# A prompt's last 16 rows as a masked whole tile of 128, and the products with the samples' states with the state moving, four side by side

## The chip, the cores and the metric

One Trainium2 chip, one of its cores. The metric is the device time of one launch in microseconds (us), the median of several runs. TensorE is called PE in the rows (PEld is its loading of the stationary operand), VectorE DVE, ScalarE ACT, GpSimd POOL, SyncE SP.

## What is computed

One inference step of a two-layer trunk with d_model 1024, for a prompt of 2048 tokens (16 learned meta tokens stand in front of it, so 2064 rows) and for 8 samples of one token each that carry states from earlier. In each layer one input projection feeds three branches, and one output projection with a LayerNorm merges them:

```
u = x @ w_in                                    # 5128 columns
A: y_rg  = RG-LRU(conv(rg_in))       * silu     # a scan over time
B: y_ret = norm(retention(q, k, v))  * silu     # 4 heads of 128
C: y_gdn = norm(gated_delta(q, k, v))* silu     # 4 heads of 128
y = LayerNorm(alpha * x + concat(y_rg, y_ret, y_gdn) @ w_out)

retention, a chunk:   o = ((q k^T) * decay) v + (q * q_dec) S ;  S = s_dec * S + (k * k_dec)^T v
gated delta, a chunk: solve (1 + A) [u, w] = [beta v, beta k e^gc] ; v' = u - w S
                      o = (q e^gc) S + att v' ;  S = S e^g + (k e^(g_last - gc))^T v'
```

A prompt starts with S = 0. A sample has its own S per head (128x128 in float32) in both branches: it needs `S^T q`, and in the delta branch `S^T k` too, and it updates S. Everything is float32; the large projections split each operand into two fp32r parts and add three products.

## The kernel before

The work of a layer is done in two superblocks (`sblock`, from L630): 1024 rows first, then 1040 rows of the prompt and the 8 samples. In each, stages K (the delta branch's keys, four heads), A, B and C run in the order of `STAGES`: a stage projects its slabs of w_in on TensorE in blocks of 512 columns (first superblock) or 384, 384 and 280 columns (second), and the scan, retention or delta work of the stage before is recorded between those matmuls by a pump. Behind both superblocks of a layer comes the output projection, row tile by row tile, and beside it the samples' work (`samples_delta`, `samples_ret`, L1135 to L1220).

Every operation goes through a recorder (`Recorder`, which emits all of them at L273, so that nearly every row of the profile shows that line and is told apart by its tiles). It sets each engine's order once, by a list schedule over estimated costs (`cost`, `order`). The order is fixed when the kernel is built: an engine whose next instruction waits holds up those behind it.

The second superblock has 1040 rows of the prompt: two groups of four tiles of 128 rows, and 16 rows that are left. `tl` (in `sblock`) lists them as `(0, 4, 128), (4, 4, 128), (8, 1, 16)`, the last number being the rows `R` of a tile. All steps of the keys, delta and retention branches slice their operands by `R`, so the products of the 16 rows run with 16 rows or 16 columns of TensorE's array: `pdt` and `pk` (`keys_bg`), `pw`, `pu`, `qk`, `pz`, `pd`, `po`, `pno` (`delta_bg`: `prep`, `chain`, `outs`, `norm`), and `qk`, `po`, `pd`, `pno` (`retention_bg`). A plain product in float32 shows as two MATMUL records (two passes), a transpose or an fp32r product as one.

In the samples' work the state of a head, `sv` (128 x 8 samples x 128), is fetched by one DMA, and for each sample its 128x128 matrix is the stationary operand and one column (retention) or two (delta) are moving: 8 products a head. There are 4 heads, 2 branches and 2 layers, so 16 such groups.

At the start SP's queue fetches the first slab `raw`, the first columns of x (`xraw`), the constants `ct`, then small tensors, and then the next slab and columns. The program gives these transfers eight semaphores in turn, so the ninth can only be issued when the first has landed.

## Time and profile before

| | |
|---|---|
| runs of the kernel before | 3144.42, 3139.70, 3141.41 us; median 3141.41 us |
| the profiled execution's own time | 3134.19 us |
| its span, first to last instruction | 3132.2 us |
| mean granted TensorE clock | 0.996 of full speed |
| busy: TensorE | 3089.2 us, 99% of the span |
| busy: VectorE, ScalarE, GpSimd | 65%, 41%, 22% |
| DMA | 262.96 MB, mean 84 GB/s |

How to read it: a share is busy time over the span. A matmul's duration in a row is its latency, and matmuls overlap; what one costs the engine is the distance from its start to the start of the next. In a timeline row "x9" are nine records in a row, its first number is the start of the first of them, and the second the time until the last one's end. Brackets give idle time before the row and what ended it.

### The profile page before, as it was taken

The page shows a single profiled execution, that of the slowest core. Times are in us where ns is not written, and L with a number is a line of the kernel's source. Part 1 is how long each engine was busy: PE and PEld are TensorE (multiplying, and loading weights), DVE is VectorE, ACT ScalarE, POOL GpSimd, SP SyncE. Part 2 cuts the span into 40 slices and gives each one's busy share as a digit, 9 for nine tenths or more (in the row PEclk, how much of TensorE's full clock was granted, in tenths as well). Part 3 has the DMA queues.
Part 4 walks back from the last instruction along what each step waited for, and adds up shares of the span by engine and source line. Part 5 has one row for each costly group of instructions (what it writes and reads, how often), then busy time and mean ns, then how long its engine had stood idle before and what let it go on. Part 6 is the DMA issues. An engine that isn't in the chain of part 4 may idle for free. (4 is left out here: it accounts for less than half of the span.)

```text
span 3132.2 us, 47396 instructions
## 1 busy us (share of the span) xinstructions
PE 3089.2 (99%) x18876; PEld 2707.9 (86%) x18876; DVE 2038.0 (65%) x3736; ACT 1294.2 (41%) x2732; POOL 678.5 (22%) x651
## 2 busy tenths in 40 slices
PE   8999999999999999999999999999999999999999
PEld 6888888899999999788778888888999999997886
DVE  6976565679756565656469765655897565656564
ACT  4455444543454454311144544444434544543100
POOL 2222132222222231011022222222222222311110
PEclk9999999999999999999999999999999999999999
DMA  4121111321111113555231212112211111136641
GB/s 154 63 70 48 57 50 58 110 82 51 49 54 59 46 57 96 179 175 168 95 115 56 70 48 66 52 57 96 85 50 50 54 59 43 61 92 195 183 145 59
DMA packets 137060, 262.96 MB, mean 84 GB/s; under 512 B 24368, under 2 KB 79600, under 8 KB 136840
## 3 DMA queue, kind: packets, MB, share of 16 engines
q1 hardware_dynamic: 113640, 179.91, 18.5%
q0 software_dynamic: 23200, 80.04, 7.1%
q8 instruction: 148, 2.42, 0.3%
q14 instruction: 72, 0.59, 0.1%
HBM read 195.13 MB, written 65.04 MB: 83 GB/s over the span
## 5 line engine op out<-in xcount | busy, mean ns | idle before, releaser
L273 PE MATMUL pj<-arena 128*128 128x512 f32 (+3 forms) x9760 | 2114.1, 360 | 14.3 <-ACT arena L273 7.6
L273 PEld LDWEIGHTS pj<-arena 128*128 128x128 f32 (+1 forms) x9760 | 1625.5, 187 | 170.6 <-ACT arena L273 8.2
L273 POOL TENSOR_TENSOR arena<-raw,arena 128x1024 fp32r<-128x1024 f32 x159 | 399.5, 2512 | 1077.5 <-ACT arena L273 886.4
L273 ACT CAST arena<-raw 128x1024 fp32r<-128x1024 f32 x180 | 189.0, 1050 | 302.4 <-PE pj L273 163.9
L273 DVE SCALAR_TENSOR_TENSOR stg<-stg,eg,pd 128x128 f32<-128x128 f32 x264 | 90.8, 344 | 117.6 <-PE pd L273 116.4
L273 PE MATMUL pj<-arena,ah 128*128 128x512 f32 x512 | 166.0, 401 | 1.3 <-ACT arena L273 1.3
L273 ACT COPY ur<-pj 128x512 f32<-128x512 f32 (+2 forms) x160 | 80.4, 503 | 146.1 <-PE pj L273 146.0
L273 ACT ACT_TABLE_LOAD x106 | 136.0, 1283 | 4.5 <-DVE vT L273 1.9
L273 ACT COPY sw<-pj 64x512 f32<-64x512 f32 (+2 forms) x160 | 79.9, 500 | 103.2 <-PE pj L273 65.7
L273 PEld LDWEIGHTS pj<-arena,ah 128*128 128x128 f32 x512 | 96.7, 189 | 24.5 <-ACT arena L273 1.8
L273 PE MATMUL pj<-arena,al 128*128 128x512 f32 (+1 forms) x296 | 111.6, 398 | 0.1
L273 ACT ACTIVATE g<-pj 128x512 f32<-128x512 f32 (+2 forms) x120 | 61.8, 515 | 109.9 <-PE pj L273 108.9
L273 PE MATMUL pd<-kv 128*128 128x128 f32 x512 | 99.9, 277 | 3.5 <-DVE kv L273 2.6
L273 PEld LDWEIGHTS pz<-stg,wq 128*128 128x128 f32 x512 | 89.7, 189 | 12.5 <-DVE stg L273 2.7
L273 PE MATMUL pz<-stg,wq 128*128 128x128 f32 x512 | 99.6, 276 | 0.8 <-DVE stg L273 0.4
L273 PEld LDWEIGHTS pd<-kv 128*128 128x128 f32 x512 | 86.8, 190 | 13.7 <-issue 2.8
L273 DVE SCALAR_TENSOR_TENSOR g<-g,pj 128x512 f32<-128x512 f32 (+2 forms) x120 | 69.5, 579 | 39.5 <-ACT g L273 38.5
L273 ACT ACTIVATE wq<-pz,eg 64x128 f32<-64x128 f32 x128 | 44.1, 361 | 122.9 <-DVE kv L273 55.1
L273 PE MATMUL po<-arena,ah 128*128 128x512 f32 x288 | 93.9, 400 | 0.0
L273 ACT CAST bh<-mb 128x512 fp32r<-128x512 f32 x32 | 19.6, 620 | 171.3 <-PE po L273 107.9
L273 DVE SCALAR_TENSOR_TENSOR qT<-ur,gcw,qT 128x1024 f32<-128x1024 f32 (+1 forms) x48 | 75.0, 1562 | 18.4 <-ACT qT L273 18.3
L273 DVE SCALAR_TENSOR_TENSOR kT<-ur,gcw,kT 128x1024 f32<-128x1024 f32 (+1 forms) x48 | 74.0, 1541 | 19.2 <-ACT kT L273 18.7
(388 smaller groups left out, 5057.7 us busy)
## 6 DMA issues: line engine op xcount, KB each, us to landing
raw<-in_win SPq DMA_DIRECT2D x160, 512.0 KB, 3.3
ma<-mix_d SPq DMA_DIRECT2D x31, 512.0 KB, 5.1
mix_d<-g POOLq DMA_DIRECT2D x24, 520.0 KB, 3.3
mix_d<-g POOLq DMA_DIRECT2D x24, 512.0 KB, 3.4
raw<-in_wout SPq DMA_DIRECT2D x24, 512.0 KB, 4.4
xr<-in_x SPq DMA_DIRECT2D x16, 512.0 KB, 5.1
x_d<-yo POOLq DMA_DIRECT2D x16, 512.0 KB, 3.3
sv<-row_d POOLq DMA_DIRECT2D x16, 512.0 KB, 4.7
```

The source lines that it names most:

```text
L273: return lambda *args, **kw: self._r.note(self._n, op, lambda: f(*args, **kw), args, kw)
```

## The change

The 16 rows become a tile of 128 that ends with the prompt, so its first 112 rows repeat rows of the second group and must count for nothing. `tl` now carries a tile's first column (`np_ - 128` for the last). New constants in `cl` do the masking: `tmask` (1 for the last 16 rows) on the gates `gg` and `bt`, `tkdec` and `tdec` for retention's decays, `teps` for its epsilon; they are filled by two memsets on GpSimd and four small DMAs on SP's queue. The delta branch takes the last tile's second half chunk only (`q.cis = (1,)`), whose two products with the state (`wt` and `qT`) become one of 128 columns. Only the last 16 columns of the result are written.

In the samples' work `from_state` makes 32 columns (the needed one or two, and neighbours that are not used) stationary and the state moving, at output partitions 0, 32, 64 and 96 in turn; ScalarE copies the 128x256 result out of PSUM, two transposes bring the columns back, and the rest is as before.

```diff
+    cl = cst.tile([128, 13], F32, name="cl")
+    tmask, tkdec, tdec, teps = cl[:, 0:1], cl[:, 1:5], cl[:, 5:9], cl[:, 9:13]
+
+    def tail_constants():
+        G.memset(cl[:, 0:9], 0.0)
+        G.memset(teps, EPS)
+        a = _C["dret"][0] + 127
+        for dst, src in ((tmask, const[0:16, _C["ones"][0]:_C["ones"][1]]),
+                         (tkdec, const[0:16, _C["kdect"][0]:_C["kdect"][1]]),
+                         (tdec, const[0:16, a:a + 385:128]),
+                         (teps, const[0:16, _C["epsr"][0]:_C["epsr"][1]])):
+            SP.dma_start(dst[112:128], src)
...
-            tl = [(0, 4, 128), (4, 4, 128)] + ([(8, 1, 16)] if samp else [])
+
+
+            tl = [(0, 4, 0), (4, 4, 512)] + ([(8, 1, np_ - 128)] if samp else [])
...
-                    V.tensor_tensor(gg, gg, C("valid").unsqueeze(2).to_broadcast([128, 9, 4]), op=OP.mult)
+                    V.tensor_tensor(gg[:, 8], gg[:, 8], tmask.to_broadcast([128, 4]), op=OP.mult)
...
+                    V.tensor_tensor(bt[:, 8], bt[:, 8], tmask.to_broadcast([128, 4]), op=OP.mult)
...
-                        PE.matmul(pd[:R, :nt, :m], m1r[:R, :R], x[:R, :nt, :m], start=(e == 0), stop=False)
-                    PE.matmul(pd[:R, :nt, :m], identb[:R, :R],
-                              negb[:R, :m].unsqueeze(1).to_broadcast([R, nt, m]), start=False, stop=True)
-                    A.activation(dt[:R, t4:t4 + nt, :m], pd[:R, :nt, :m], AF.Exp)
+                        PE.matmul(pd[:, :nt], m1r, x[:, :nt], start=(e == 0), stop=False)
+                    PE.matmul(pd[:, :nt], identb, negb.unsqueeze(1).to_broadcast([128, nt, 64]), start=False, stop=True)
+                    A.activation(dt[:, t4:t4 + nt], pd[:, :nt], AF.Exp)
...
-                        for o in range(0, R, 64):
-                            c0 = (t4 + i) * 128 + o
-                            PE.matmul(pk[o:o + m, i, :m], kT[:, c0:c0 + m], kT[:, c0:c0 + m],
-                                      start=True, stop=True)
-                    if R == 128:
+                        for o in (0, 64):
+                            cc = slice(c0 + i * 128 + o, c0 + i * 128 + o + 64)
+                            PE.matmul(pk[o:o + 64, i], kT[:, cc], kT[:, cc], start=True, stop=True)
+                    if nt == 4:
                         V.tensor_tensor(ap[:, t4:t4 + 4, h, :], pk, dt[:, t4:t4 + 4], op=OP.mult)
                     else:
-                        V.tensor_tensor(apt[:16, :, h], pk[:16, 0, :16], dt[:16, 8, :16], op=OP.mult)
+                        V.tensor_tensor(apt[:, :, h], pk[96:128, 0, 48:64], dt[96:128, 8, 48:64], op=OP.mult)
...
-                        q.wt, q.at = small("wt", [128, 16]), small("at", [16, 16])
+                        q.wq, q.at, q.cis = gs[0].wq, gs[0].at, (1,)
...
+                        A.copy(ttbd[96:128, 0, 112:128], apt[:, :, h])
+                        G.memset(ttbd[96:128, 0, 96:112], 0.0)
+                        G.tensor_copy(q.wq[:, 0, 2], qT[:, c0 + 64:c0 + 128])
...
-                        PE.matmul(pw[:, i, :R], kk[:R, 0, i], inv_t(i), start=True, stop=True)
-                    if R == 128:
+                        PE.matmul(pw[:, i], kk[:, 0, i], ttbd[:, i], start=True, stop=True)
+                    if nt == 4:
                         A.copy(q.wq[:, :, 0:4:3], pw.rearrange("p t (e c) -> p t e c", e=2))
 
                         G.tensor_copy(kk[64:128, 0], kk[64:128, 1])
                         G.memset(kk[0:64, 0], 0.0)
                         G.memset(kk[64:128, 1], 0.0)
                     else:
-                        A.copy(q.wt, pw[:, 0, :R])
+                        A.copy(q.wq[:, 0, 3], pw[:, 0, 64:128])
...
-                        for ci, (o, n) in enumerate(((0, 64), (64, 64)) if q.R == 128 else ((0, 16),)):
+                        for ci in q.cis:
                             pz = q.pz[i // 2][:, i % 2, ci]
-                            if q.R == 128:
-                                PE.matmul(pz, q.wq[:, i, 2 * ci:2 * ci + 2].rearrange("p e c -> p (e c)"), S,
-                                          start=True, stop=True)
-                            else:
-                                PE.matmul(pz[:16], q.wt, S, start=True, stop=True)
-                                PE.matmul(q.pz[0][:16, 0, 1], qT[:, q.c0:q.c0 + 16], S, start=True, stop=True)
-                            if q.R == 128:
-
-                                V.tensor_tensor(uv[o:, 1, i], uv[o:, 0, i], pz[o:], op=OP.add)
-                            else:
-                                V.tensor_tensor(uv[:n, 1, i], uv[:n, 0, i], pz[:n], op=OP.add)
+                            PE.matmul(pz, q.wq[:, i, 2 * ci:2 * ci + 2].rearrange("p e c -> p (e c)"), S,
+                                      start=True, stop=True)
+
+                            o = 64 * ci if nt == 4 else 0
+                            V.tensor_tensor(uv[o:, 1, i], uv[o:, 0, i], pz[o:], op=OP.add)
                             yield
                             ps = p1("pd")
-                            if q.R == 128:
-                                PE.matmul(ps[:, :128], kk[:, 1 - ci, i], uv[:, 1, i], start=True, stop=True)
-                            else:
-                                PE.matmul(ps[:, :128], kk[:n, 1, i], uv[:n, 1, i], start=True, stop=True)
+                            PE.matmul(ps[:, :128], kk[:, 1 - ci, i], uv[:, 1, i], start=True, stop=True)
...
-                        PE.transpose(pn[:, i, :R], q.o[:R, i], C("swap") if R == 128 else ident[:R, :R])
-                    gv = g[:, c0:c0 + nt * R].rearrange("p (t c) -> p t c", t=nt)
-                    V.scalar_tensor_tensor(out=gv, in0=pn[:, :nt, :R], scalar=VV("nw"), in1=gv,
-                                           op0=OP.mult, op1=OP.mult)
-                    yield
-
-                gs = [alloc(i) for i in range(len(tl))]
+                        PE.transpose(pn[:, i], q.o[:, i], C("swap"))
+                    if nt == 4:
+                        gv = g[:, c0:c0 + 512].rearrange("p (t c) -> p t c", t=4)
+                    else:
+                        pn, gv = pn[:, 0, 112:128], g[:, np_ - 16:np_]
...
+            def from_state(pb, sv, cols, c0, n):
+                pr = pt("psv").rearrange("p (s c) -> p s c", s=4)
+                for b in range(NS):
+                    j = 32 * (b % 4)
+                    PE.matmul(pr[j:j + 32, b // 4], cols[:, c0 + n * b:c0 + n * b + 32], sv[:, 0, b], start=True, stop=True)
+                rw = wk.tile([128, 2, 128], F32, tag="gm", name="rw", bufs=2)
+                A.copy(rw, pr[:, 0:2])
+                for s in range(2):
+                    PE.transpose(pb[:, 128 + 128 * s:256 + 128 * s], rw[:, s], ident)
+                return pb[:, 128:384].rearrange("p (b e) -> p b e", e=32)
...
-                    for b in range(NS):
-                        PE.matmul(pb[:, 16 + 2 * b:18 + 2 * b], sv[:, 0, b], kq[:, h, b], start=True, stop=True)
-                    pv = pb[:, 16:32].rearrange("p (b e) -> p b e", e=2)
+                    pv = from_state(pb, sv, swork, 16 * h, 2)
...
-                    for b in range(NS):
-                        PE.matmul(pb[:, b:b + 1], sv[:, 0, b], qs[:, h, b:b + 1], start=True, stop=True)
-                    V.scalar_tensor_tensor(out=o[:, h], in0=pb[:, 0:8], scalar=GAM[h], in1=o[:, h],
+                    pv = from_state(pb, sv, scol.rearrange("p c e h b -> p (c e h b)"), 128 + 8 * h, 1)
+                    V.scalar_tensor_tensor(out=o[:, h], in0=pv[:, :, 0], scalar=GAM[h], in1=o[:, h],
...
-                        PE.matmul(pa[:R, i, :R], kT[:, cc], qT[:, cc], start=True, stop=True)
-                    V.tensor_tensor(sn[:R, 0, :nt, :R], pa[:R, :nt, :R],
-                                    dret[:R, h, :R].unsqueeze(1).to_broadcast([R, nt, R]), op=OP.mult)
+                        cc = slice(c0 + i * 128, c0 + i * 128 + 128)
+                        PE.matmul(pa[:, i], kT[:, cc], qT[:, cc], start=True, stop=True)
+                    if q.last:
+                        V.scalar_tensor_tensor(out=sn[:, 0, 0], in0=pa[:, 0], scalar=tdec[:, h:h + 1],
+                                               in1=C("minc"), op0=OP.mult, op1=OP.mult)
+                    else:
+                        V.tensor_tensor(sn[:, 0, :nt], pa[:, :nt],
+                                        dret[:, h].unsqueeze(1).to_broadcast([128, nt, 128]), op=OP.mult)
...
-                    kd = C("kdec" if R == 128 else "kdect")[:R, h:h + 1]
-                    A.activation(kv[:R, 0, :nt], pk[:R, :nt], AF.Copy, scale=kd)
+                        PE.transpose(pk[:, i, :], kT[:, c0 + i * 128:c0 + i * 128 + 128], ident)
+                    kd = (tkdec if q.last else C("kdec"))[:, h:h + 1]
...
-                        PE.matmul(po[:R, i], qT[:, cc], S, start=False, stop=True, skip_group_check=True)
+                        cc = slice(c0 + i * 128, c0 + i * 128 + 128)
+                        PE.matmul(po[:, i], qT[:, cc], S, start=False, stop=True, skip_group_check=True)
                         ps = p1("pd")
-                        PE.matmul(ps[:, :128], kv[:R, 0, i], kv[:R, 1, i], start=True, stop=True)
-                        V.scalar_tensor_tensor(out=S, in0=S, scalar=GAM[h] ** R, in1=ps[:, :128],
+                        PE.matmul(ps[:, :128], kv[:, 0, i], kv[:, 1, i], start=True, stop=True)
+                        V.scalar_tensor_tensor(out=S, in0=S, scalar=GAM[h] ** (16 if q.last else 128), in1=ps[:, :128],
                                                op0=OP.mult, op1=OP.add)
...
-                        PE.transpose(pn[:, i, :R], q.sn[:R, 1, i], ident[:R, :R])
-                    nv = q.sn[:, 0, :nt, :R]
-                    A.activation(nv, pn[:, :nt, :R], AF.Identity, scale=VV("gnw")[:, h:h + 1],
-                                 bias=VV("gnb")[:, h:h + 1])
-                    gv = g[:, c0:c0 + nt * R].rearrange("p (t c) -> p t c", t=nt)
+                        PE.transpose(pn[:, i], q.sn[:, 1, i], ident)
+                    nv, pn = q.sn[:, 0, :nt], pn[:, :nt]
+                    gv = g[:, q.c0:q.c0 + nt * 128].rearrange("p (t c) -> p t c", t=nt)
+                    if q.last:
+                        nv, pn, gv = nv[:, 0, 112:128], pn[:, 0, 112:128], g[:, np_ - 16:np_]
```

Two places in TensorE's order and one in SP's. First the delta branch's chain of the 16 rows, first head of layer 0, where `kv`/`attb` rows belong to the second group of tiles, `pj` to the projections, and `tk` holds the 16 rows' keys and values. Before:

```order
L273 MATMUL pd<-kv_1099 128x128
L273 MATMUL po<-kv_1099,attb_102 128x128
L273 MATMUL pj<-arena 128x384 x4
L273 MATMUL pz<-stg_103,wt 16x128
L273 MATMUL pz<-stg_103,qT 16x128
L273 MATMUL pj<-arena 128x280 x5
L273 MATMUL pd<-tk 128x128
L273 MATMUL po<-tk,at 16x128
```

Now:

```order
L273 MATMUL pd<-kv_1099 128x128
L273 MATMUL po<-kv_1099,attb_103 128x128
L273 MATMUL pj<-arena 128x384
L273 MATMUL pj<-arena 128x280 x4
L273 MATMUL pz<-stg_104,wq 128x128
L273 MATMUL pj<-arena 128x280 x6
L273 MATMUL pd<-tk 128x128
L273 MATMUL po<-tk,attb_102 128x128
```

Two `pz` products of 16 columns are one of 128, and the last product gives 128 rows instead of 16; the place in the order is nearly the same.

Second, the first delta group of the samples in layer 0, on TensorE, between matmuls of the output projection (`wh`, `arena`, `ah`, `al`). Before:

```order
L273 MATMUL pj<-arena,ah 128x512
L273 MATMUL ps_1716<-swork,ct 128x8
L273 MATMUL ps_1716<-swork,sv 128x2 x8
L273 MATMUL pj<-arena,ah 128x512
L273 MATMUL pj<-arena,al 128x512
```

Now:

```order
L273 MATMUL pj<-arena,ah 128x512
L273 MATMUL ps_1703<-swork,ct 128x8
L273 MATMUL psv<-sv,swork 32x128 x8
L273 MATMUL pj<-arena,ah 128x512
L273 MATMUL pj<-arena,al 128x512
L273 MATMUL pj<-arena,ah 128x512 x2
L273 MATMUL ps_1703<-ct,rw 128x128 x2
```

Eight products of two moving columns are eight of 128 moving columns for 32 result rows; four matmuls later two transposes follow, which need ScalarE's copy `rw`.

Third, the head of SP's queue. Before:

```order
L273 DMA cb<-in_convb 128x384 [waits DMAHW0_49]
L273 DMA h_121<-in_rgh 128x32 [waits DMAHW1_49]
L273 DMA rab<-in_wab 128x64 [waits DMAHW2_49]
L273 DMA wgt<-in_wg 128x256 [waits DMAHW3_49]
L273 DMA raw<-in_win 128x1024 [waits DMAHW4_49,DVE_49]
L273 DMA xraw<-in_x0t 128x2x512 [waits DMAHW5_49,DVE_49]
```

Now:

```order
L273 DMA wgt<-in_wg 128x256 [waits DMAHW3_49]
L273 DMA cl<-in_const 16x1 [waits DMAHW4_49,Pool_49]
L273 DMA cl<-in_const 16x4 [waits DMAHW5_49]
L273 DMA cl<-in_const 16x4x1 [waits DMAHW6_49]
L273 DMA cl<-in_const 16x4 [waits DMAHW7_49,Pool_49]
L273 DMA raw<-in_win 128x1024 [waits DMAHW0_49,DVE_49]
L273 DMA xraw<-in_x0t 128x2x512 [waits DMAHW1_49,DVE_49]
```

The four loads of `cl` stand ahead of the second slab, which now waits for the transfer `cb` (DMAHW0) and, through the loads before it, for `ct`, `vt` and `fb` (DMAHW5 to 7); before, it waited for the fourth `xraw` (DMAHW4).

## Rows read from the trace of the kernel before

**Rows 1.** The page's first part: busy time, share, instructions.

```profile
PE 3089.2 (99%) x18876; PEld 2707.9 (86%) x18876; DVE 2038.0 (65%) x3736; ACT 1294.2 (41%) x2732; POOL 678.5 (22%) x651
```

**Rows 2.** Timeline of PE, 748.5 to 756.4: start us, us, what.

```profile
751.50 0.38 PE L273 MATMUL pd<-kv 128*128 128x128 f32 x2
...
751.86 1.82 PE L273 MATMUL pj<-arena 128*128 128x384 f32 x9
753.60 0.39 PE L273 MATMUL po<-str,qT 128*16 128x128 f32 x2
...
754.34 2.32 PE L273 MATMUL pj<-arena 128*128 128x384 f32 x13
```

**Rows 3.** Timeline of PE, 889.8 to 895.1: the delta branch, first head.

```profile
889.89 0.38 PE L273 MATMUL pz<-stg,wq 128*128 128x128 f32 x2
890.03 0.60 PE L273 MATMUL pj<-arena 128*128 128x384 f32 x2
890.56 0.39 PE L273 MATMUL pw<-tth,tk 16*128 16x16 f32 x2
890.88 0.44 PE L273 MATMUL pj<-arena 128*128 128x384 f32 x1
```

**Rows 4.** Timeline of PE, 911.5 to 915: the delta chain of the 16 rows.

```profile
912.81 0.39 PE L273 MATMUL pz<-stg,wt 128*16 128x128 f32 x2
...
913.35 0.92 PE L273 MATMUL pj<-arena 128*128 128x280 f32 x5
914.21 0.48 PE L273 MATMUL pd<-tk 16*128 16x128 f32 x2
...
914.93 0.40 PE L273 MATMUL pj<-arena 128*128 128x280 f32 x1
```

**Rows 5.** Timeline of PE, 768 to 769.5: retention's transposes back, last tile.

```profile
768.64 0.38 PE L273 MATMUL pj<-arena 128*128 128x280 f32 x1
768.95 0.23 PE L273 MATMUL pno<-ct,tk 16*128 16x16 f32 x1
769.11 0.65 PE L273 MATMUL pj<-arena 128*128 128x280 f32 x3
```

**Rows 6.** Timeline of PE, 1320 to 1327: one group of the samples' products.

```profile
1323.29 1.93 PE L273 MATMUL ps<-swork,sv 128*128 128x2 f32 x16
1325.07 0.48 PE L273 MATMUL pj<-arena,ah 128*128 128x512 f32 x1
1325.39 0.39 PE L273 MATMUL pj<-arena,al 128*128 128x512 f32 x1
1325.62 0.62 PE L273 MATMUL pj<-arena,ah 128*128 128x512 f32 x2
```

**Rows 7.** Timeline of PE, 46.5 to 49.5: products at 64 columns, two side by side.

```profile
48.52 0.69 PE L273 MATMUL pk<-kT 128*64 128x64 f32 x16
49.13 0.73 PE L273 MATMUL pj<-arena 128*128 128x512 f32 x2
```

**Rows 8.** Timeline of PE, 200.2 to 202.1: 32x32 products of two groups.

```profile
201.70 0.21 PE L273 MATMUL pg<-tn,ap 32*32 32x32 f32 x1
...
201.79 0.19 PE L273 MATMUL pg<-tt,gt 32*32 32x32 f32 x1
```

**Rows 9.** Timeline of PE, 1272 to 1280; then the windows view of 1277 to 1287.3.

```profile
1278.29 0.56 PE L273 MATMUL ps<-scol,sv 128*128 128x1 f32 x2 [4.33 <-DMA sv<-in_sret]
...
1277.00:1287.30 10.30, 9.01 (x28) 7.78 (x29) 7.79 (x7) 3.41 (x3) 0.00 (x0) 0.50 0.63 192
```

**Rows 10.** Timelines of SP, ACT, DVE and PE, from 0 to 45 us.

```profile
10.77 0.33 SPq L273 DMA_DIRECT2D raw<-in_win  x1
...
12.84 0.21 ACT L273 ACTIVATE nea<-fb 128x4 f32<-128x4 f32 x1 [1.07 <-DMA fb<-in_fbc]
...
17.14 4.26 DVE L273 SCALAR_TENSOR_TENSOR sp<-sp 128x4 f32<-128x4 f32 x8
...
22.66 12.51 PE L273 MATMUL pj<-arena 128*128 128x512 f32 x43 [2.74 <-DVE arena L273]
```

More of the change, by code (lines that the diff above doesn't have):

```diff
@@ L401, in pj, with pz2 @@
         return psum.tile([128, 512], F32, tag="pj", name="pj", bufs=2)
-    def pz2():
+    def pz2(n=2):
         return [psum.tile([128, 512], F32, tag="pz", name="pz", bufs=2).rearrange("p (t c) -> p t c", t=4)
-                for _ in range(2)]
+                for _ in range(n)]
     def p1(tag):
@@ L710, in gates_c @@
                 pg = pt("gt")[:, :144].rearrange("p (t e) -> p t e", e=16)
-                if samp:
-                    G.memset(gtok[:, 8], 0.0)
                 for t in range(NT):
-                    n = min(128, ts - t * 128)
-                    PE.transpose(pg[:n, t, :], gab[:16, t * 128:t * 128 + n], ident[:16, :16])
-                for n, ta, tb in ((128, 0, 8), (24, 8, 9))[:1 + samp]:
-                    V.tensor_copy(gtok[:n, ta:tb], pg[:n, ta:tb, 0:8])
-                    V.tensor_tensor(gtok[:n, ta:tb], gtok[:n, ta:tb], pg[:n, ta:tb, 8:16], op=OP.add)
+                    c0 = min(t * 128, np_ - 128)
+                    PE.transpose(pg[:, t, :], gab[:16, c0:c0 + 128], ident[:16, :16])
+                V.tensor_copy(gtok[:, :NT], pg[:, :NT, 0:8])
+                V.tensor_tensor(gtok[:, :NT], gtok[:, :NT], pg[:, :NT, 8:16], op=OP.add)
                 V.tensor_tensor(xa[:, :NT], gtok[:, :NT, 0:4],
@@ L875, in inverses @@
                     pn = pt("pn")
-                    PE.transpose(pn[:4, :16], nf[:16, 32:36], ident[:16, :16])
-                    A.copy(nbt, pn[:4, :16])
+                    PE.transpose(pn[:4, :128], nf[:, 32:36], ident)
+                    A.copy(nbt, pn[:4, 112:128])
                     a_ = a_[:, :16]
@@ L883, in inverses @@
                     yield
-                    yield from solve(a_, nbt, t_, prod, 4, 16)
+                    yield from solve(a_[:, :, 16:], nbt, t_, prod, 4, 16, 16)
                     V.transpose(out=apt, in_=t_[:32])
@@ L999, in prep @@
                     for i in range(nt):
-                        PE.matmul(pu[:R, i], inv_t(i), uv[:R, 0, i], start=True, stop=True)
-                    A.copy(uv[:R, 0, :nt], pu[:R, :nt])
+                        PE.matmul(pu[:, i], ttbd[:, i], uv[:, 0, i], start=True, stop=True)
+                    A.copy(uv[:, 0, :nt], pu[:, :nt])
                     yield
@@ L1097, in delta_bg @@
                 pq = pt("psw")
[L1098 to L1099 removed]
+                PE.matmul(pq[:, :NT], C("swap"), ssq[:, :NT], start=True, stop=True)
+                V.tensor_copy(ssq[:, :NT], pq[:, :NT])
                 V.tensor_scalar(ssq[:, :NT], ssq[:, :NT], 4.0 * 128.0 * EPS, 4.0 * 128.0 * EPS * EPS,
@@ L1296, in prep @@
                     for i in range(nt):
-                        PE.transpose(pv[:R, i, :], vT[:, c0 + i * 128:c0 + i * 128 + R], ident)
-                    A.copy(kv[:R, 1, :nt], pv[:R, :nt])
+                        PE.transpose(pv[:, i, :], vT[:, c0 + i * 128:c0 + i * 128 + 128], ident)
+                    A.copy(kv[:, 1, :nt], pv[:, :nt])
                     yield
                 def chain(q):
-                    t4, nt, R, c0, kv, sn, po = q.t4, q.nt, q.R, q.c0, q.kv, q.sn, q.po
+                    t4, nt, c0, kv, sn, po = q.t4, q.nt, q.c0, q.kv, q.sn, q.po
                     for i in range(nt):
-                        PE.matmul(po[:R, i], sn[:R, 0, i, :R], kv[:R, 1, i], start=(i == 0), stop=False,
+                        PE.matmul(po[:, i], sn[:, 0, i], kv[:, 1, i], start=(i == 0), stop=False,
                                   skip_group_check=True)
@@ L1326, in retention_bg @@
                     yield from chain(gs[1])
-                V.tensor_scalar(rs[:, :NT], mv[:, :NT, 1], C("epsr")[:, h:h + 1], None, op0=OP.add)
+                V.tensor_scalar(rs[:, :8], mv[:, :8, 1], C("epsr")[:, h:h + 1], None, op0=OP.add)
+                if samp:
+                    V.tensor_scalar(rs[:, 8:9], mv[:, 8:9, 1], teps[:, h:h + 1], None, op0=OP.add)
                 A.activation(rs[:, :NT], rs[:, :NT], AF.Sqrt)
```

142 lines of the change are left out of this document (64 added, 78 removed).

## The prediction

> **What bounds the kernel now.** I read the page's busy times first, then timelines of TensorE around the places that the change touches, then the start and the one long wait there. TensorE is busy for 3089.2 of 3132.2 us while VectorE, ScalarE and GpSimd have 65%, 41% and 22% [rows 1]. So nearly every us that leaves TensorE's stream leaves the time, and work added to another engine costs only where TensorE waits for it. A busy share does not say what a product costs, as matmuls overlap; that is read from start to start. Three unit prices follow. A projection step of 512 columns is 0.23 us (1325.39 to 1325.62 [rows 6]), so I estimate 0.17 for 384 columns and 0.126 for 280. A float32 pass costs 0.112: sixteen take 1.78 [rows 6], although each moves only two columns. And a product on part of the array costs more than its passes: its neighbours are held up before and after it.
>
> **The 16 rows, TensorE.** There are 4 heads in 2 layers, so 8 of each of the following.
> In retention's chain a full tile's pair (751.50 to 751.86) takes 0.36 for four passes, the 16 rows' pair (753.60 to 754.34) 0.74. The nine steps between them take 1.74 where nine at 0.174 are 1.57; about 0.08 of the rest follows the float32 pair, as it would anyway, and 0.09 stands before the small pair [rows 2]. In the full form the pair costs what the other does: 0.47 less, 3.8 us in all.
> In the delta chain, 912.81 to 914.93 is 2.12 us with five steps of 280 columns (0.63), so 1.49 belong to eight passes; with 0.09 of entry 1.58. The change makes one product of `wt` and `qT`, so six passes are left, 0.67. That is 0.91 each, 7.3 us [rows 4].
> A single small product: `pw` takes 0.32 (890.56 to 890.88) where a full two-pass one takes 0.14 (889.89 to 890.03), and the two steps before it take 0.53 instead of 0.35, of which again 0.08 is usual: 0.27 too much [rows 3]. `pw`, `pu` and retention's `po` are three such kinds: 24 times 0.27, 6.5 us. The sixteen `qk` have 16 moving columns now and will have 128, so part of the gain is given back; I take half, 0.14: 2.2 us.
> The transposes back, `pno`: 768.64 to 768.95 is 0.31 for one step of 0.126, and the transpose itself 0.16 [rows 5]. Instead of 0.34, with the next step held up as well, it will be one pass of 0.112; with 0.1 for that step 0.33 each, sixteen: 5.3 us.
> The keys' three `pdt` products lose a switch of the array and gain columns, and `pk` gains a product that mostly joins its neighbours of the same form: 0.2 together, 1.6 us.
> Sum: 3.8 + 7.3 + 6.5 + 2.2 + 5.3 + 1.6 = 26.7. Bounds: 20, if a third of what I call switching is something else and stays; 31, if the `qk` gain all.
>
> **The samples' products, TensorE.** Before: 16 groups of 1.78, 28.5 us [rows 6]. Now eight products of 32 stationary and 128 moving columns at four places of the array, then two transposes. No row shows four at once. The nearest: products of 64 columns at two places, sixteen records from 48.52 to 49.13 [rows 7]. One 64-column pass is half of 0.112, so sixteen in a line would take 0.90; the row has 0.61 with a switch in it, and two side by side give 0.45 plus that switch. So two places overlap fully. If four do, a group needs two rounds of two passes, 4 x 0.112 = 0.45. I add 0.4 for switching (0.16 inside the row just read, 0.24 in the neighbours, as above) and 0.22 for two transposes: 1.07. Saved: 0.71 a group, 11.4 us. The bounds: 16 times 1.63 if two run at a time, 16 times 2.41 if none do. I take four, since the two places of rows 7 both stream all 128 partitions without slowing each other.
>
> **What else is moved.** The copy `rw` is 256 columns on ScalarE, ahead of the transposes by four steps, 0.93 us. ScalarE is busy for 3.4 of 10.3 us even in the crowded stretch of [rows 9], so I cost it at nothing; if a 1 us cast stands before it each time, it would be 0.5 to 1 us a group.
> On VectorE and GpSimd the 16 rows' operations get more partitions and hardly more elements each, plus some copies and memsets; VectorE's 65% covers them.
> The four small loads on SP's queue stand ahead of the second slab. It is issued at 10.77 now; then only after `ct`, `vt`, `fb` and `cb` have landed. ScalarE gets `fb` at 12.84, so about 13.6: 2.8 later. Behind it are the other columns of x, on which TensorE waits at 22.66. But VectorE is the late one: its eight little operations from 17.14 take 4.26 us, beside GpSimd's split of the slab [rows 10]. If the slab comes later they run before that split, and VectorE gets to the columns no later. Between 0 and 2.8 I take 0.5.
> SP's later orders have one `dt` load instead of two, which gains nothing on TensorE. The wait of 4.33 us for the first state at 1278.29, and the 10.3 us at a granted clock of 0.50 (1.2 of 2.4 GHz) that include it [rows 9], stay: the first `psv` stands at the same place, and its load on the same queue.
>
> **The sum.** 26.7 + 11.4 - 0.5 = 37.6 us less. The profiled execution took 3134.2, 7.2 under the median of the runs shown, 3141.4. I set the sum against that execution, 3096.6, and add the 7.2 for the median: **3103.8 us**, 1.2% less. A measurement of this kernel can tell about 0.2% (6 us) from no change.
>
> **Rivals.**
> *Two at a time.* Each product is two passes at one place; if passes start strictly in the order of the program, a second pass holds back the next product, and only it and one neighbour overlap: nine slots of 0.112. A group is 1.01 + 0.4 + 0.22 = 1.63, the samples save 2.4, and the time is 3112.8. For it: rows 7 fit two as well as four. Against it: at 201.70 a `tn,ap` product starts while a pass of the earlier `tt,gt` products starts only at 201.79 [rows 8], so a product did pass one that stood before it. The Trainium skill, "TensorE: Matmul & The Clock Gate", Part 3 (The mechanism), says that matmuls start and end in program order with no reordering; by that rule this rival holds, and rows 8 speak against it. Chance 0.22.
> *None side by side.* The change then doesn't do what it says: sixteen passes of 0.112 plus the rest, 2.41 a group, 10 us more than before; 3125.2. Against it: the overlap of rows 7. Chance 0.07.
> *No wait for the first state.* With other moments of transfer the 4.33 us and the half clock behind them (half of 9.0 busy us is 4.5) may go: 3095. Or they may come a second time: 3112.6. The order gives no reason for either. Chance 0.05 for the first; the second lies within the range.
> *A slower kernel: the clock.* If the narrow groups drew the clock down for 10.3 us each time, as in [rows 9], a group would cost 4.5 us more. It decides from nine of the sixteen groups (37.6 / 4.5); with all sixteen the time is 3176. Against it: the clock of 0.50 comes after an idle wait, and sixteen passes of two columns run at 0.112 in [rows 6], the full rate. Chance 0.02.
>
> **How the numbers follow.** The forecast has 0.62, the rivals 0.36, and 0.02 goes to what I don't see, such as TensorE's gain eaten by its waits for other engines. The forecast's own range is 3096 to 3111 (20 to 31 for the rows, 0 to 2.8 for the start, and the runs' spread of 5 us). Taking in the first two rivals and the missing wait it is 3093 to 3125. Faster by over 0.2%: 0.62 + 0.22 + 0.07 + 0.05 less a little for sums of mishaps, 0.94. Slower: the clock and something more, 0.03. Same: 0.03.
>
> **What would show it.** Right: no rows of 16 partitions or columns among `pz`, `po`, `pd`, `pw`, `pu`, `qk`; the steps before them without the extra 0.09; `psv` in sixteen passes within about 0.55 us, and the first transposes without a wait. Two at a time: `psv` in about 1.0 us; none: 1.8. The start: TensorE at 22.66 or up to 2.8 later. The sum is wrong if the second superblocks are not some 13 us shorter each, or if TensorE's idle time grows by more than a few us.

## The result, and the profile after

| | before | after |
|---|---|---|
| runs, us | 3144.42, 3139.70, 3141.41, 3143.85 | 3096.30, 3097.44, 3101.23, 3102.70 |
| median | 3142.63 | 3099.34 |
| profiled execution | 3134.19 | 3096.30 |

The ratio on record is 0.9874, with a 95% interval of 0.9852 to 0.9895. By the two medians shown it is 43.3 us less (a ratio of 0.9862, inside the interval), by the two profiled executions 37.9. Forecast were 3103.8 and 37.6. That the second figure fits so well is partly luck: several of its parts were off, and the errors cancel. This section shows the rows; the account stands behind the experiments.

Page of the changed kernel, busy times, against [rows 1]:

```profile
PE 3051.0 (99%) x18908; PEld 2692.0 (87%) x18908; DVE 2048.9 (66%) x3758; ACT 1298.1 (42%) x2740; POOL 692.2 (22%) x649
```

TensorE's busy time fell by 38.2 us, as the span did (37.7). Where it fell is read from the windows view, cut at the first and last step of the two second superblocks, in which the 16 rows are worked. Its columns are the window, its length, then busy time and count of PE, PEld, DVE, ACT and POOL, then the granted clock, DMA share and GB/s. Before:

```profile
594.67:1251.64 656.97, 650.67 (x4645) 617.91 (x4644) 440.88 (x917) 309.06 (x708) 157.50 (x158) 1.00 0.20 65
2159.14:2818.91 659.77, 654.55 (x4695) 621.21 (x4694) 443.56 (x921) 309.69 (x711) 153.38 (x148) 1.00 0.20 65
```

After:

```profile
594.45:1242.54 648.09, 638.89 (x4646) 620.37 (x4645) 446.29 (x925) 307.37 (x705) 164.80 (x160) 1.00 0.20 66
2134.61:2785.74 651.13, 644.01 (x4696) 625.75 (x4695) 446.54 (x929) 308.02 (x707) 161.21 (x150) 1.00 0.20 65
```

The superblocks are 8.9 and 8.6 us shorter, not 13 each. TensorE's busy time fell by 11.8 and 10.5, its idle time (length less busy) rose from 6.3 to 9.2 and from 5.2 to 7.1 us. So part of what left its stream came back as waiting. The same view of the stretches behind the two superblocks, with the output projections and the samples' work, before and then after:

```profile
1251.64:2159.14 907.50, 896.69 (x4816) 738.90 (x4815) 574.87 (x952) 340.49 (x663) 184.31 (x166) 0.99 0.30 97
2818.91:3132.20 313.29, 303.75 (x1387) 242.69 (x1385) 177.27 (x285) 50.56 (x86) 32.35 (x57) 0.99 0.48 146
```

```profile
1242.54:2134.61 892.07, 886.26 (x4832) 725.95 (x4831) 575.95 (x955) 343.62 (x672) 183.57 (x162) 1.00 0.31 100
2785.74:3094.50 308.76, 298.13 (x1404) 232.75 (x1402) 178.97 (x288) 54.51 (x94) 32.13 (x57) 1.00 0.49 150
```

Here TensorE's busy time fell by 10.4 and 5.6 us; its idle time fell by 5.0 and rose by 1.1.

The places of [rows 2 to 6] in the changed kernel, from PE's timeline: retention's chain of the 16 rows, `pw`, the delta chain, `pno`, and one group of the samples.

```profile
752.41 0.38 PE L273 MATMUL po<-str,qT 128*128 128x128 f32 x2
...
752.77 3.56 PE L273 MATMUL pj<-arena 128*128 128x384 f32 x19
...
888.61 0.59 PE L273 MATMUL pj<-arena 128*128 128x384 f32 x2
889.04 0.38 PE L273 MATMUL pw<-ttbd,tk 128*128 128x128 f32 x2
889.18 0.60 PE L273 MATMUL pj<-arena 128*128 128x384 f32 x2
...
911.37 0.38 PE L273 MATMUL pz<-stg,wq 128*128 128x128 f32 x2
911.51 1.03 PE L273 MATMUL pj<-arena 128*128 128x280 f32 x6
912.37 0.38 PE L273 MATMUL pd<-tk 128*128 128x128 f32 x2
912.59 0.39 PE L273 MATMUL po<-tk,attb 128*128 128x128 f32 x2
912.73 2.57 PE L273 MATMUL pj<-arena 128*128 128x280 f32 x17
...
770.17 0.27 PE L273 MATMUL pno<-ct,tk 128*128 128x128 f32 x1
770.20 6.02 PE L273 MATMUL pj<-arena 128*128 128x280 f32 x36
...
1304.80 0.65 PE L273 MATMUL psv<-sv,swork 128*32 128x128 f32 x16
1305.38 0.50 PE L273 MATMUL pj<-arena,ah 128*128 128x512 f32 x1
...
1306.41 0.38 PE L273 MATMUL ps<-ct,rw 128*128 128x128 f32 x2
1306.54 0.48 PE L273 MATMUL pj<-arena,al 128*128 128x512 f32 x1
1306.86 0.63 PE L273 MATMUL pj<-arena,ah 128*128 128x512 f32 x2
```

Retention's pair takes 0.36 us (752.41 to 752.77) where [rows 2] had 0.74. `pw` takes 0.14 instead of 0.32, and the two steps ahead of it 0.43 instead of 0.53, 0.35 and the usual 0.08. The delta chain takes 1.36 with six steps of 0.126, so 0.60 is left of the 1.49 of [rows 4]. A `pno` takes 0.03 instead of 0.16. These are about the forecast's prices. A group of the samples takes 0.58 instead of the 1.78 of [rows 6], and its two transposes 0.13 and 0.09 more in the step behind them (0.32 instead of 0.23).

Where TensorE waits: total us, times, longest. Before, three rows that grew:

```profile
PE pj L273 <- DVE g L273: 3.0, 4, 0.7
PE pd L273 <- DVE kv L273: 2.6, 6, 0.5
PE pz L273 <- DVE stg L273: 0.4, 2, 0.2
```

After, with two that are new:

```profile
PE pj L273 <- DVE g L273: 4.7, 6, 1.0
PE psv L273 <- DMA sv<-in_sret: 3.6, 2, 2.7
PE pd L273 <- DVE kv L273: 3.4, 6, 1.0
PE pz L273 <- DVE stg L273: 1.9, 4, 0.7
PE ptv L273 <- DVE sn L273: 1.8, 2, 0.9
```

The rows on VectorE grew by 5.8 us together, at about the idle time that the two superblocks gained (4.8). The first state is still waited for, 0.95 us in layer 0 and 2.7 in layer 1; the single wait of 4.33 in [rows 9] is gone, and so is the half clock behind it:

```profile
1264.00:1271.00 7.00, 6.05 (x38) 3.96 (x38) 5.64 (x8) 3.97 (x6) 1.65 (x1) 1.00 0.81 274
2794.00:2812.00 18.00, 15.21 (x83) 11.32 (x81) 14.57 (x16) 13.76 (x18) 2.51 (x2) 1.00 0.85 263
```

Both windows contain one of the waits, and the granted clock is 1.00 in both (2.4 GHz), against 0.50 in [rows 9].

### The profile page after: what moved, and what is told of

Same layout as the page of the kernel before. It is cut to its first block, busy times and chain, and to the rows that moved or that the text cites. A ratio compares the mean times of both kernels' runs of the same rounds, so it can differ in the third digit from the quotient of the medians.

```text
span 3094.5 us, 47507 instructions
## 1 busy us (share of the span) xinstructions
PE 3051.0 (99%) x18908; PEld 2692.0 (87%) x18908; DVE 2048.9 (66%) x3758; ACT 1298.1 (42%) x2740; POOL 692.2 (22%) x649
## 5 line engine op out<-in xcount | busy, mean ns | idle before, releaser
L273 DVE SCALAR_TENSOR_TENSOR vT<-ur,gcw,vT 128x1024 f32<-128x1024 f32 (+1 forms) x48 | 77.9, 1623 | 10.5 <-ACT vT L273 10.0
L273 DVE TENSOR_TENSOR kv<-kv,pz 128x128 f32<-128x128 f32 (+1 forms) x128 | 37.0, 289 | 71.4 <-PE pz L273 70.7
```

The lines of the kernel that those rows point to most:

```text
L273: return lambda *args, **kw: self._r.note(self._n, op, lambda: f(*args, **kw), args, kw)
```

## The experiments

The theory after the result: TensorE's work shrank about as forecast, the samples' products run side by side at four places, and the missing gain of the rows lies in new waits. Against it stood: prices that were too high, two at a time, and a gain that is only the vanished wait.

### One part at a time

The whole tile alone (the two calls of `from_state` undone), and the samples alone:

```diff
-                    pv = from_state(pb, sv, swork, 16 * h, 2)
+                    for b in range(NS):
+                        PE.matmul(pb[:, 16 + 2 * b:18 + 2 * b], sv[:, 0, b], kq[:, h, b], start=True, stop=True)
```

> The changed kernel with the samples' products as they were before (8 stationary states, one or two moving columns); the 16 rows keep the whole masked tile. Theory A (from the two traces, second superblocks 8.9 and 8.6 us shorter, start 1.0 later): 16.5 us less than before, 3126. Theory B (the prediction's own terms, 26.7 for the rows less 0.5 for the start): 26.2 less, 3116. The second superblocks tell the two apart in the trace: 8 to 9 us shorter each by A, about 13 by B.

> The kernel before with the samples' products alone changed (32 columns stationary, the state moving, four places, copy, two transposes). Theory A: a group costs about 0.8 us and two transposes 0.22, instead of 1.78, so 12 us less, 3130.6; 3126 if the wait for the first state goes as well. Rival, two at a time: 2.4 us less, 3140. Rival, none side by side: 10 us more, 3153.

Measured: the rows alone 3112.08, 0.9933 (0.9913 to 0.9954); the samples alone 3117.12, 0.9944 (0.9926 to 0.9962); before, beside them on the same chip, 3138.29. By these ratios that is 21 and 18 us, by the medians 26.2 and 21.2, and both intervals are wide, because runs of the kernel before spread from 3127.29 to 3141.73: at a mean granted clock of 0.998 they take 3127.29 to 3128.11, at 0.994 or 0.995 3138.29 to 3141.73, in between 3130.43 to 3141.34. One execution of each kernel is traced, so what differs between the runs is argued from the clock: that the wait for the first state, with the half clock behind it, comes in some and not in others. Two kernels below with the samples' old form don't settle it: retention alone is traced in its fastest run (3124.36) and waits 0.2 us for that state, delta alone waits 3.5 us with 6.8 us at half clock behind and is 1.4 us above its fastest. The fastest runs of each, which would leave it out, are 3127.29 before, 3108.29 with the rows alone (19.0 less), 3115.01 with the samples alone (12.3 less). The two add up to 31.3; with both parts the fastest run there took 3096.09, 31.2 less (the kernel of "The start" below, which stands in for the changed one: its trace has the same loads in the same order). So the parts are additive. The interval for the rows alone, 14 to 27 us, holds 16.5 and 26.2 both; the second superblocks of its trace tell more:

```profile
595.00:1241.73 646.73, 637.36 (x4645) 618.91 (x4644) 445.83 (x925) 307.11 (x705) 164.98 (x160) 1.00 0.20 66
2143.38:2796.12 652.74, 645.68 (x4695) 627.20 (x4694) 446.62 (x929) 307.62 (x707) 161.11 (x150) 0.99 0.20 65
```

They are 10.2 and 7.0 us shorter than before. In the first the kernel before has 3.4 us at half clock (632.00 to 635.40) and this one none; in the second this one has 6.8 us (2182.60 to 2189.40) and the one before none. At full clock these would have taken half as long, so without them the gain is 8.5 and 10.4 us, together 19.0: 23.9 us of work left TensorE, and 4.9 of idle time came. So neither 16.5 nor 26.2 was right for the rows, and two at a time (2.4) and none side by side (slower) fell.

In the kernel with the rows alone the first state's wait shows what follows it in the samples' old form, PE's timeline and then the windows view:

```profile
1266.63 0.35 PE L273 MATMUL ps<-scol,sv 128*128 128x1 f32 x2 [2.09 <-DMA sv<-in_sret]
...
1267.80:1274.60 6.80, 6.80 (x22) 5.75 (x22) 3.49 (x5) 1.60 (x2) 0.00 (x0) 0.50 0.77 238
```

After an idle 2.09 us come 6.8 us at 0.50. In the changed kernel 2.7 us of idle were followed by none; a kernel below has both the new form and a half clock behind 2.93 us of idle, so the form alone does not decide.

### Four places, or two, or the order

```diff
-                for b in range(NS):
+                for b in (0, 4, 1, 5, 2, 6, 3, 7):
                     j = 32 * (b % 4)
```

> The changed kernel with the eight products of a group in another order: samples 0, 4, 1, 5, 2, 6, 3, 7, so that two neighbours stand at the same place of the array. Same work, same result. Theory A (a pass waits only for its own place, so a later product at a free place goes ahead): two products of two passes at each of four places, still about 0.57 us a group, and the time is that of the changed kernel, 3099, within 3 us. Rival (passes start strictly in the order of the program, and the alternation of places made the overlap): each place's four passes stand in a line and only the last one overlaps with the next place's first, 13 slots of 0.112 or 1.46 us, 0.9 more in each of 16 groups: 3114.

Measured: 3098.40, 0.9888 (0.9868 to 0.9907), no different from the 3099.34 of the changed kernel or the 3099.58 of its stand-in beside it. One group, and the step behind it:

```profile
1305.99 0.67 PE L273 MATMUL psv<-sv,swork 128*32 128x128 f32 x16
1306.58 0.50 PE L273 MATMUL pj<-arena,ah 128*128 128x512 f32 x1
```

0.59 us instead of 0.58. A product at a free place does not wait for the passes that stand ahead of it at a busy one. The rule of the Trainium skill, "TensorE: Matmul & The Clock Gate", Part 3 (The mechanism), that matmuls start and end in program order, by which 1.46 us were expected, does not hold for products at different places here.

```diff
-                    j = 32 * (b % 4)
+                    for a, z in ((32, 64), (64, 128)):
+                        V.memset(pr[a:z, 0:2], 0.0)
...
+                    j = 0
```

> The changed kernel with all eight products of a group at output partitions 0 to 31, so that they write over one another (the samples' results are left out of the account); two small memsets on VectorE fill the partitions that nothing writes. Theory A (the gain is four places side by side): the sixteen passes stand in a line, 1.8 us at 0.112 each, up to 2.6 at the 0.16 of a small pass, instead of 0.57: 20 to 32 us more than the changed kernel, 3119 to 3131. Rival (a pass of 32 stationary columns is short by itself): about 0.6 us a group, 3099.

Measured: 3117.76, 0.9959 (0.9945 to 0.9974), 18 us more than the changed kernel, which was not run beside it.

```profile
1308.89 1.94 PE L273 MATMUL psv<-sv,swork 128*32 128x128 f32 x16
1310.75 0.50 PE L273 MATMUL pj<-arena,ah 128*128 128x512 f32 x1
```

1.86 us a group, 0.116 a pass: at one place the narrow form gains nothing over [rows 6]. The whole gain is four places at once, and 16 times the difference of 1.28 is 20.5 us.

### The start

```diff
-    tail_constants()
     for l in range(DEPTH):
...
+                if i_st == 1 and l + sb == 0:
+                    tail_constants()
```

> The changed kernel with the four small loads of the masks recorded later, inside the first superblock, so that SP's queue starts as it did before; TensorE's order is the same. Theory A (the loads in front of the second slab put off its transfer and so the split and TensorE's columns): TensorE goes on at 22.7 us instead of 23.6, and the time is 1.0 us less, 3098. Rival (the eight small operations on VectorE are the late ones in any case): TensorE goes on at 23.6 again, no change.

Measured: 3099.58, 0.9889 (0.9869 to 0.9909). But the edit did not move the loads: the scheduler set them ahead of the second slab again. SP's queue in this kernel, and where TensorE's wait for the second columns ends:

```profile
10.12 2.99 SPq L273 DMA_DIRECT2D cl<-in_const  x4
13.21 0.37 SPq L273 DMA_DIRECT2D raw<-in_win  x1
...
23.88 2.50 PE L273 MATMUL pj<-arena 128*128 128x512 f32 x5 [2.72 <-DVE arena L273]
```

So this run repeats the changed kernel and tests neither theory. The traces of the other kernels do, as some have the loads in front of the slab and some have no such loads. With them the slab is issued at 13.92 in the changed kernel, and at 13.36, 13.80 and 13.86 with the rows, retention or delta alone; TensorE goes on at 23.62, 23.01, 22.77 and 22.61. Without them the slab is issued at 10.77 before and at 11.18 with the samples alone; TensorE goes on at 22.66 and 23.54. The slab comes about as much later as forecast (2.8), but the moment at which TensorE goes on scatters by 1 us, and not with the loads: they cost nothing that can be seen, and the expectation of 1.0 was read out of scatter.

### Retention or delta alone

Two mixed kernels take `retention_bg`, or the keys and the delta branch, from the changed kernel and the rest from the one before, as in

```diff
-                    q.t4, q.nt, q.R = tl[gi]
+                    q.t4, q.nt, q.c0 = ((0, 4, 0), (4, 4, 512), (8, 1, np_ - 128))[gi]
```

> The kernel before with the masked whole tile in the retention branch alone (keys, delta and samples as before). Theory A (the stages of the second superblocks that hold retention's work are 2.75 us shorter each layer in the changed kernel's trace): 5.5 us less than before, the four stretches behind B0 to B3 shorter by 0.2 to 1.1 us each, the others unchanged. Theory B (the prediction's terms: chain 3.8, po 2.2, half of qk 1.1, half of pno 2.65): 9.8 less, 1.2 in each of the eight.

> The kernel before with the masked whole tile in the keys and the delta branch alone (retention and samples as before). Theory A (from the changed kernel's trace: keys nothing, the stretches with delta's work 6.8 us shorter a layer): 13.5 us less than before. Theory B (the prediction's terms: chain 7.3, pw and pu 4.3, half of qk 1.1, half of pno 2.65, keys 1.6): 17 less.

Measured: retention 3134.34, 0.9998 (0.9985 to 1.0011), delta 3123.41, 0.9978 (0.9963 to 0.9993). By these ratios that is 1 and 7 us, which fits neither theory, and together far less than the 19 of both. The second superblocks of the kernel with retention alone, and a row of its waits:

```profile
594.81:1249.47 654.66, 645.46 (x4645) 617.75 (x4644) 441.54 (x918) 308.08 (x709) 157.62 (x154) 1.00 0.20 65
2147.07:2807.82 660.75, 652.29 (x4695) 624.10 (x4694) 443.22 (x922) 307.78 (x711) 153.91 (x144) 1.00 0.19 64
...
PE qk L273 <- ACT kv L273: 5.7, 3, 2.7
```

TensorE's busy time fell by 5.2 and 2.3 us, and its idle time rose by 2.9 and 3.2, most of it a wait for ScalarE's `kv` that is 5.7 us here, 1.0 before and 0.6 with both parts. With delta alone the same windows give 8.8 and 7.4 us less busy time, and 3.1 and 2.2 more idle. What half clock costs (half of its length) has to be taken out of these: neither kernel has the 3.4 us that the kernel before has in the first superblock, and retention alone has 3.4 us in the second (2383.70 to 2387.10). That leaves 3.5 and 4.0 for retention, 7.1 and 7.4 for delta. So the work of the parts nearly adds up, 7.5 and 14.5 against 24.0 with both, somewhat under the priced 9.8 and 17; the idle time does not, 6.1 and 5.3 against 4.8. That is where the missing gain went: each order that the scheduler makes has waits of its own. What in the order makes each wait was not tried. (The times say less than this; their runs spread as those of the kernel before do, from 3124 to 3140 with retention alone.)

### The price of a small product

Behind each state product `pd` of a full tile in the delta branch of the kernel before stands one more product that nobody uses: a small one of 16 moving columns, a whole one, or a small one of 128 moving columns, 256 of them in a launch.

```diff
                                 PE.matmul(ps[:, :128], kk[:, 1 - ci, i], uv[:, 1, i], start=True, stop=True)
+                                PE.matmul(ps[:16, 128:144], kk[:16, 1 - ci, i, :16], uv[:16, 1, i, :16], start=True, stop=True)
```

> The kernel before with one extra product of 16 rows by 16 columns by 16, whose result nobody uses, behind each product that updates the delta branch's state for a full tile: 2 superblocks x 2 layers x 4 heads x 16 = 256 extra float32 products in the small form, each between whole-array neighbours. It is compared with the twin that has a whole product there. Theory A (in the changed kernel's trace pw, pu and po went from 0.32 to 0.14 us, and their neighbours hardly gained): the small one costs 0.18 to 0.20 us more than the whole one, 46 to 51 us over all. Theory B (the prediction's unit price of a switch to the small form and back, 0.27): 69 us more than the twin. By itself it is slower than before by 256 times 0.3 to 0.5, 77 to 128 us.

> The same 256 extra products, each 128 by 128 by 128, unused too. Both theories: two passes of 0.112 us each, 57 us slower than before, or down to 36 us if two passes of the same form as their neighbours cost the 0.14 that the whole pw shows from start to start; the difference from the small twin is what tells the theories apart (46 to 51 against 69 us).

> As the run with 256 extra small products, but each of the small products (16 rows by 16 columns) moves 128 columns instead of 16. That run cost 84 us more than before and its whole twin 63, so a small product of 16 moving columns cost only 0.08 to 0.11 us more than a whole one. Theory A (a switch of form costs about 0.11; the rest of the gain that pw, pu and po showed is the price of small passes with 128 columns, 0.317 us for two where 16 by 16 takes 0.14): 0.18 us more each than with 16 columns, 130 us slower than before, 3263. Theory B (the switch is the whole price, the columns don't matter): 84 us again, 3217.

Measured: 3216.76, 1.0270 (1.0243 to 1.0296); 3195.43, 1.0191 (1.0165 to 1.0217); 3255.18, 1.0399 (1.0371 to 1.0427). Over before that is 84, 63 and 125 us, or 0.33, 0.25 and 0.49 for one. The four passes (the `pd` and the extra one) and the steps behind, in the kernels with the whole, the small and the wide small product:

```profile
270.61 0.61 PE L273 MATMUL pd<-kv 128*128 128x128 f32 x4
270.98 1.16 PE L273 MATMUL pj<-arena 128*128 128x512 f32 x4
```

```profile
267.73 0.53 PE L273 MATMUL pd<-kv 128*128 128x128 f32 x4
268.19 0.97 PE L273 MATMUL pj<-arena 128*128 128x512 f32 x3
```

```profile
270.76 0.70 PE L273 MATMUL pd<-kv 128*128 128x128 f32 x4
271.39 0.96 PE L273 MATMUL pj<-arena 128*128 128x512 f32 x3
```

0.37, 0.46 and 0.63 us. So a small product costs 0.08 to 0.09 more than a whole one if it moves 16 columns, and 0.24 to 0.26 if it moves 128. The theory of 0.18 to 0.20 fell, and so did a switch that is the whole price. The forecast's 0.27 holds within a tenth for a small product that moves 128 columns, as `po` does; of a product that holds 128 columns and moves 16, as `pw` does, no such run was made. The forecast's 0.14 for `qk`, with 16 columns on both sides, was somewhat high.

### Taking the wait for the first state away

First one more step of the pump between its fetch and its product; then the same by the scheduler's reckoning of the fetch.

```diff
                     G.dma_start(sv[:, 0], sret[l, h])
                     yield
+                    if h == 0:
+                        yield
```

> The changed kernel with one more step of the pump between the fetch of retention's first state and its first product, so that the product stands some 8 to 10 us later in TensorE's order. Theory A (TensorE's two waits for that state, 0.95 and 2.7 us, and the chance of a half-clock stretch behind them are all that is left of the old 4.3 us wait): 3 to 4 us less than the changed kernel, 3096, and a narrower spread of the runs. Rival (the samples' chain gets longer, and the row tile behind it, or the first state of the delta branch, is waited for instead): no change or a few us more.

```diff
-                end = max(dma, start + 1.6) + 0.3
+                end = max(dma, start + 1.6) + 0.3 + op.late
```

(`op.late` is 3.5 for GpSimd's loads into SBUF, else 0.)

> The changed kernel with one number of the scheduler changed: it reckons GpSimd's loads of states (and of the rows beside them) as landing 3.5 us later, so that TensorE's first group of products stands right ahead of its transposes, which keep their place, instead of some 80 rows of the order earlier; the other groups move by one to four matmuls and the rest of TensorE's order is the same. Theory A (the waits of 0.95 and 2.7 us for the first states cost what they last, and nobody needs that group's products earlier): 3 to 4 us less than the changed kernel, 3096, with no wait for a state. Rival (as in the run with the extra step, the wait comes back at later states): 3099 to 3104.

Measured: 3104.44, 0.9924 (0.9900 to 0.9948), and 3104.32, 0.9913 (0.9894 to 0.9931): some 5 us slower than the changed kernel, each. It was not run beside them; the kernel before was, and took no longer there (medians 3130.17 and 3132.19) than beside the first experiments. The extra step moved the first group much farther than the expected 8 to 10 us, from 1266.97 to 1308.48; the scheduler's reckoning moved it to 1300.77. In the first kernel TensorE waits 6.8 us for states, four times, and 3.8 us for ScalarE's `ah`. PE's timeline of the second, last group of retention in layer 0 and in layer 1:

```profile
1400.57 0.65 PE L273 MATMUL psv<-sv,scol 128*32 128x128 f32 x16 [1.16 <-DMA sv<-in_sret]
...
2947.44 1.08 PE L273 MATMUL psv<-sv,scol 128*32 128x128 f32 x16 [2.93 <-DMA sv<-in_sret]
```

The rival holds in both: the first group no longer waits, later states are late instead, and TensorE waits for ScalarE's `ah` (2.9 us in the second kernel), which it does not in the changed kernel. The group behind the 2.93 us took 1.08 instead of 0.65: it ran at half clock (0.50 from 2947.30 to 2950.70). No kernel tried beats the changed one by more than its runs spread.

## Why the prediction was right, and where it was not

Account of the two profiled executions, whose spans differ by 37.7 us:

| part | forecast | found | from |
|---|---|---|---|
| 16 rows, TensorE's work | 26.7 | 24.0 | busy time of the two superblocks, 11.8 + 10.5, and 1.7 for 3.4 us at half clock in layer 1 after |
| 16 rows, new waits | 0 | -4.8 | idle time of the two superblocks |
| samples' products | 11.4 | 11.5 | busy time behind the superblocks, 10.4 + 5.6, less 4.5 for half clock before |
| waits for the first states | 0 | 0.7 | 4.3 before, 0.95 + 2.7 after |
| other waits behind the superblocks | 0 | 3.2 | idle time there, 5.0 - 1.1, less the 0.7 |
| half clock | 0 | 2.8 | half of the 9.0 busy us of [rows 9], less the 1.7 above |
| the start | -0.5 | 0.2 | the first of the two superblocks begins at 594.67 and 594.45 |
| sum | 37.6 | 37.6 | |

The 3.4 us at half clock in layer 1 of the changed kernel lie inside its second superblock, where the kernel before has none:

```profile
2173.80:2177.20 3.40, 3.40 (x12) 3.38 (x12) 3.01 (x10) 1.79 (x6) 0.00 (x0) 0.50 0.31 125
```

In layer 0 both kernels have such a stretch, so it drops out (631.00 to 634.40 after). Before:

```profile
632.00:635.40 3.40, 3.40 (x12) 3.40 (x11) 1.65 (x5) 1.91 (x5) 0.53 (x1) 0.51 0.03 5
```

No wait stands in the 10 us ahead of 632.00 or of 2173.80. Sixteen `gs` products on 16 rows of the array do, from 629.06 before and from 2172.17 after; whether they bring the half clock on was not tried.

**The 16 rows.** Together the prices were right within about a tenth: the chains, `pw`, `pu` and `po` as forecast, `pno` 0.25 (0.16 and two held-up steps of about 0.1 before, 0.03 and the usual 0.08 now) instead of 0.33. What failed is the step "VectorE's 65% covers them". VectorE's operations for the tile are not many, but TensorE's order is fixed, and at single places `g`, `kv`, `stg` and `sn` came later than the product that needs them: 4.8 us. The forecast had named this only as a mishap without a size. The keys' 1.6 I could not find in the rows.

**The samples.** The mechanism, four places side by side, was right, and so was the total, but not its parts. "I add 0.4 for switching" was too much: a delta group takes 0.58 with its switch in it, the `ps` ahead of it 0.07 more than before (0.21 from 1304.59, where it took 0.14 from 1323.15), the step behind it no more, so a group saves 0.9 and not 0.71. But retention's groups took 1.70 before (1352.81 to 1354.51), not 1.78, have 0.1 more ahead of them now and save 0.8, and the first of each layer, which other products cut in two, 0.4. These rows add up to 12.7, near the 12.3 between the fastest runs of the samples alone; where the busy time's 11.5 loses the rest the rows do not show. That a pass of 64 columns costs half of 0.112, from which the forecast read the full overlap of two places in [rows 7], no row or run shows; the overlap of four is shown by the group's 0.58 against the 1.86 at one place. `rw` was late once, by 0.3 us.

**The wait and the clock.** "Stay" was wrong. The first product stands at the same place, but its load, issued at 1269.75 before and 1261.3 after, let it start 8.5 us later before and 5.7 after. The rival with 3095 named the event; its chance of 0.05 was too low: the kernel before has runs of 3122.6 to 3128.1 too, where those shown were 3139 to 3144. Between the fastest runs the change is worth 31.2 us, 6.4 less than forecast; between the first medians 43.3. The forecast of 37.6 lies between, and 3103.8 came out only 4.5 from the median. In the account too the 37.6 comes out only with 6.7 us that the forecast did not have: the clock, the first states and the other waits. That is the luck in it.

**The rivals.** Two at a time and none side by side fell by the group's 0.58 us and by the kernel with one place. The slower clock fell: the granted clock is 1.00 in the two windows above, beside the first groups of both layers, and from 1242.54 to 1480.00 and from 2785.74 to 3090.00, which hold all sixteen groups. The argument against it, that the clock of 0.50 comes after an idle wait, was not sound: the stretch at 632.00 has none ahead of it, and stood in the kernel before.

## What to carry to other kernels

Price a product by start to start with its neighbours on both sides: on part of the array a product with 128 columns held or moved (`pw` holds them, `po` moves them) costs 0.24 to 0.28 us more than on the whole array, one with 16 on both sides some 0.1. Where an order is fixed when the kernel is built, an engine at 99% gives back some of each gain in waits of a microsecond at new places: a fifth of it here. Look at how a kernel's runs spread, and at the clock beside each, before taking one profile as the base of a sum; the work that left TensorE in a stretch is read only after its half clock is taken out. And where a scheduler sets the order, see in the trace whether an edit moved what it was meant to move.

## What I had not expected of the hardware

Sixteen passes at four places of the array take 0.58 us in either order of the program, 1.86 at one place: passes go ahead of others that stand before them. A small product of 16 by 16 with 16 moving columns costs 0.08 to 0.09 us more than one of the whole array, with 128 moving columns 0.24 to 0.26. And taking a wait of 0.95 and 2.7 us away left two kernels some 5 us slower, not faster, as other waits came in their place.
